# Hymba decoder layer: the first down-projection weights prepared inside the last FFN reading, the residual moved to the last block of pairs

## The chip, the cores and the metric

One core of a Trainium2 chip runs the whole layer. The metric is device time in microseconds (us), the median of some runs. TensorE (PE) multiplies, with its own weight loads (PEld) beside it; VectorE (DVE) and ScalarE (ACT) work on tiles; GpSimd (POOL) and SyncE (SP) here mainly issue DMA transfers, each from a queue in order.

## The reference, cut to what matters

1024 prompt tokens, 32 sample tokens and 16 meta tokens go through one layer: a mixer (short convolution and retention), then a SwiGLU FFN of width 2816, then a norm. The change lies in the FFN's down projection:

```python
x = x + jnp.concatenate([conv_out, ret_out], axis=-1) @ w_out
xn = _rmsnorm(x, norm2_g)
x = x + (jax.nn.silu(xn @ w_gate) * (xn @ w_up)) @ w_down      # w_down: 2816 x 1024
...
y_prompt = _rmsnorm(xp, final_norm_g)[:, N_META:]
```

`x` on the right of the second sum is called the residual here.

## The kernel before, in words

Everything is fp32, with features on the partitions and tokens along the free axis. The 1056 tokens that go through the FFN are two sets `s` (544 and 512), each of two groups `g`; group 0 of both sets together is 528 columns, and so is group 1. A matmul operand is split in two: a rounded high half (`whi`, `hh`, made by ACT as a copy to fp32r) and the rest (`wlo`, `hl`, made by DVE as a subtraction). A product then takes three matmuls per 128x128 weight tile: high by high, high by low, low by high. `split_u` splits weights into four rotating `whi` and four `wlo` buffers, so a split waits for the product four before it.

`strassen` multiplies a 2 x 2 block matrix of weights (a11, a12; a21, a22) by a 2 x 2 block matrix of activations with seven products instead of eight. Its weight sums are s3 = a11 + a21, s1 = a21 + a22, s2 = s1 + a11, s4 = s2 + a12 (the signs lie in the activations). The products are called y1 (a11 with b11), z1 (s3 with t3), y2 (s2 with t2), w1 (a12 with b21), y3 (s1 with t1), z2 (a22 with t4), y4 (s4 with b22). Three PSUM tiles y, z and u collect them: y2, y3 and y4 add into y, z2 into z. After each product the callback `on(step, ps)` reads the sum so far, so y2 can't start before the reading of y1 is done, y3 not before that of y2, y4 not before that of y3, z2 not before that of z1. In a matmul's name the PSUM tile is `by`, `bz`, `bw` in the FFN and `dy`, `dz`, `dw` in the down projection; `hb` and `ht` are the activations b11, b21, b22 and t1 to t4.

The FFN is read in 22 readings f, one for each 128 of its features: gate and up are the two rows, the token groups the two columns, and a product is 24 matmuls. Its `on` puts the parts together in `gt` and `up`; after the seven products ACT does Silu of `gt` and DVE multiplies by `up`. Results of readings 0 to 17 are combined in pairs and written to `hd` in DRAM, those of 18 to 21 (`spill_plain`) to `hp`; these writes are issued by POOL while the next reading runs, those of reading 21 after it.

The down projection takes the 18 paired tiles in four blocks of 2, 2, 2 and 3 pairs of them (`DBLOCKS`, `bi` 0 to 3). In a block, four calls of `strassen` follow each other, for output tiles m, m + 1 with m = 0, 2, 4, 6; a "pair" in this document is one such call. A product is 12 matmuls in blocks 0 to 2 and 18 in block 3. `x1[m][g]` are the 16 output tiles of 128 x 528 in SBUF. Before the change they hold the residual first: four are pulled when reading 21 begins, twelve during block 0, and all seven steps of each pair are DVE additions or subtractions into them:

```python
x = x1[m + i][g]
V.tensor_tensor(x, x, ps, ALU.subtract if i else ALU.add)
advance(ahead, step_n)
```

Activations are pulled from `hd` by SP (`pull_block`), one block ahead, a few with each step (`advance`); block 0's are pulled during reading 21, four with each of its steps. They lie in 62 `u` tiles of the pool `rows`, of which the FFN's own activations hold 56 until the product of reading 21 that reads them last is done. Weights come through `load_w` into five `wraw` buffers, on the same SP queue. After block 3 the four plain tiles are added in eight steps a group (`pd`), and the final norm follows.

The order on each engine is set by a scheduler that goes by the order of the code and by when it reckons buffers free; each queue then runs in that order, and an instruction that waits holds all behind it on its engine.

Of the kernel before, what the change touches and what calls it, by code (L numbers as in the profile page):

```python
# [10 lines left out]
F32 = mybir.dt.float32  # L11
F32R = mybir.dt.float32r
# [4 lines left out]
P = 128  # L17
# [101 lines left out]
def _body(nc, tc, t, offs, ncols):  # L119
# [3 lines left out]
    with contextlib.ExitStack() as ctx:  # L123
# [663 lines left out]

        def strassen(pool, a11, a21, a22, a12, n, kt, rhs, name, on):

            def total(nm, a, b):  # L790
                x = pool.tile([P, 512], F32, tag="ws", name=nm, bufs=4 if n > 384 else 2)
                V.tensor_tensor(x[:, :n], a[:, :n], b[:, :n], ALU.add)
                return x

            y, z, u = bank(name + "y"), bank(name + "z"), bank(name + "w")

            def product(ps, w, key, first):
                hi, lo = split_u(w, n)
                for s in range(SETS):
# [6 lines left out]

            product(y, a11, "b11", True)
            on("y1", cols(y))
            s3 = total("s3", a11, a21)
            product(z, s3, "t3", True)  # L810
            on("z1", cols(z))
            s1 = total("s1", a21, a22)
            s2 = total("s2", s1, a11)
            product(y, s2, "t2", False)
            on("y2", cols(y))
# [6 lines left out]
            on("z2", cols(z))  # L822
            product(y, s4, "b22", False)
            on("y4", cols(y))
# [11 lines left out]
        def spill(p, b11, b12, b21, b22):  # L836
# [22 lines left out]
            yield  # L859

        def spill_plain(i, b0, b1):
            for g, b in enumerate((b0, b1)):
                to_hd(hp[i, g], b[:, :HT], "h")
                yield
# [34 lines left out]
        def advance(gen, n):  # L899
            for _ in range(n):  # L900
                next(gen, None)

        pending = iter(())
        ahead = iter(())
# [3 lines left out]
        for f in range(NFF):  # L908
# [7 lines left out]
            if f == NFF - 1:  # L916
                for i in range(2):
                    for g in range(2):
                        x1[i][g] = pull(x1d[i, g], "x1", F32)[:, :HT]
                ahead = pull_block(0)  # L920

            def on(step, ps):
                if step == "y1":
                    S.activation(gt[0][:, :HT], ps, AF.Copy)
# [6 lines left out]
                elif step == "y3":  # L931
                    V.tensor_tensor(up[1][:, :HT], ps, up[1][:, :HT], ALU.add)
                elif step == "z2":
                    V.tensor_tensor(up[0][:, :HT], ps, up[0][:, :HT], ALU.add)
                else:
                    V.tensor_tensor(gt[1][:, :HT], ps, rstd2[1], ALU.mult)
                if f == 0 and step in ("y2", "w1"):
# [29 lines left out]
        for bi, (p0, p1) in enumerate(DBLOCKS):  # L967
# [13 lines left out]
            for m in range(0, KT, 2):  # L981
                w = nk * P
                at = 2 * p0 * P
                a11, a21 = (load_w(t["w_down"][m + i][:, at:at + w], w) for i in range(2))
                a22, a12 = (load_w(t["w_down"][m + i][:, at + w:at + 2 * w], w) for i in (1, 0))
                if bi == 0 and m > 0:
                    for i in range(2):
                        for g in range(2):
                            x1[m + i][g] = fin.tile([P, HT], F32, name=f"x1_{m + i}_{g}")
                            D.dma_start(x1[m + i][g], x1d[m + i, g])  # L990

                def on(step, ps):
                    i, g = {"y1": (0, 0), "z1": (1, 1), "y2": (1, 0), "w1": (0, 0), "y3": (1, 1), "z2": (1, 0),
                            "y4": (0, 1)}[step]
                    x = x1[m + i][g]
                    V.tensor_tensor(x, x, ps, ALU.subtract if i else ALU.add)  # L996
                    advance(ahead, step_n)

                strassen(fin, a11, a21, a22, a12, w, nk, dn_rhs, "d", on)

# [115 lines left out]
```

## Time and profile before

| | us |
|---|---|
| median of 3 runs | 1208.18 (1207.39 to 1209.49) |
| the profiled execution's own time | 1211.24 |
| its span, first to last instruction | 1209.5 |
| reading 21 of the FFN ends, block 0 begins | 951.8 |
| the third pair of block 0 begins | 982.3 |
| block 3's second pair begins | 1099.9 |
| last product of block 3 ends | 1145.9 |

Times within the span are us from its start. In rows of the profile, `out<-in` are the tiles by the program's names, `x12` is a count, and square brackets hold the idle time before the instruction on its engine and what ended it. A row `DMA wraw<-w_down` in the chain is a time in which the chain waited for that transfer.

### The profile page before, as it was taken

The numbers are of one execution on the slowest core, as the hardware profiler recorded it, in microseconds if no ns is written. First come the engines' busy times: TensorE is split into PE (matmuls) and PEld (weight loads), VectorE is DVE, ScalarE is ACT, GpSimd is POOL, SyncE is SP. The second block draws the span as 40 slices with busy tenths as digits, with TensorE's granted clock in tenths as the row PEclk, the third lists the DMA queues.
The fourth block names the chain that finished last, engine by engine and source line by source line (L and its number), as shares of the span: only waits on it lengthen the run. The fifth ranks groups of instructions, "written<-read, shape, count | busy, mean of one in ns | idle before, by whom it ended". The sixth has DMA issues, their size and how long they took to land.

```text
span 1209.5 us, 22838 instructions
## 1 busy us (share of the span) xinstructions
PE 1191.2 (98%) x8921; PEld 1138.3 (94%) x8921; DVE 843.8 (70%) x1591; ACT 487.7 (40%) x932; POOL 121.9 (10%) x251
## 2 busy tenths in 40 slices
PE   9999999999999999999999999999999899999997
PEld 8998988999989998899999999999999899999996
DVE  5455467676654577877887878787776588887656
ACT  7356531121233466545443444444444222222363
POOL 0100112000000012102211221122021000000000
PEclk9999999999999999999999999999999999999999
DMA  6221211100111355425434542454254998965213
GB/s 242 74 96 35 79 37 62 36 27 27 40 46 44 99 181 186 155 72 187 152 109 141 183 156 94 156 178 158 82 189 136 377 341 281 307 219 183 77 38 107
DMA packets 82059, 162.91 MB, mean 135 GB/s; under 512 B 10702, under 2 KB 23776, under 8 KB 81952
## 3 DMA queue, kind: packets, MB, share of 16 engines
q1 hardware_dynamic: 67424, 114.55, 29.1%
q0 software_dynamic: 14384, 46.88, 10.7%
q8 instruction: 70, 1.15, 0.4%
q14 instruction: 37, 0.30, 0.1%
q10 hardware_dynamic: 144, 0.02, 0.0%
HBM read 113.15 MB, written 48.26 MB: 133 GB/s over the span
## 4 chain that ended last, share of the span: by engine, by line
PE 96%; DMA 2%; ACT 1%; DVE 1%; issue 0%; SPq 0%; DVEq 0%; ACTq 0%
PE by L804 21%; PE bz L804 11%; PE dy L804 8%; PE po L186 8%; PE bw L804 5%; PE pk L186 4%; PE dz L804 4%; PE ph L186 4%; PE pc L186 4%; PE pd L1037 4%; PE pg L186 4%; PE pb L186 4%; PE pq L186 4%; PE pv L186 4%; PE dw L804 2%; PE po L604 1%
## 5 line engine op out<-in xcount | busy, mean ns | idle before, releaser
L158 ACT ACTIVATE whi<-wraw 128x512 fp32r<-128x512 f32 (+2 forms) x198 | 115.7, 584 | 283.2 <-issue 60.0
L160 DVE TENSOR_TENSOR wlo<-wraw,whi 128x512 fp32r<-128x512 f32 (+2 forms) x198 | 124.3, 628 | 48.1 <-ACT whi L158 47.9
L158 ACT ACTIVATE whi<-s 128x512 fp32r<-128x512 f32 (+2 forms) x152 | 83.5, 551 | 159.5 <-PE by L804 46.1
L804 PE MATMUL by<-t,whi 128*128 128x256 f32 (+1 forms) x704 | 130.3, 284 | 0.0
L804 PE MATMUL bz<-t,whi 128*128 128x256 f32 (+1 forms) x704 | 130.1, 284 | 0.0
L804 PE MATMUL by<-b,whi 128*128 128x256 f32 (+1 forms) x704 | 129.2, 283 | 0.0
L160 DVE TENSOR_TENSOR wlo<-s,whi 128x512 fp32r<-128x512 f32 (+2 forms) x152 | 89.3, 588 | 35.5 <-ACT whi L158 34.5
L804 PEld LDWEIGHTS by<-b,whi 128*128 128x128 f32 x704 | 109.1, 188 | 0.1
L804 PEld LDWEIGHTS bz<-t,whi 128*128 128x128 f32 x704 | 109.1, 188 | 0.0
L804 PEld LDWEIGHTS by<-t,whi 128*128 128x128 f32 x704 | 108.8, 188 | 0.1
L804 PE MATMUL bz<-t,wlo 128*128 128x256 f32 (+1 forms) x352 | 100.0, 284 | 0.0
L804 PE MATMUL by<-b,wlo 128*128 128x256 f32 (+1 forms) x352 | 100.0, 284 | 0.0
L804 PE MATMUL by<-t,wlo 128*128 128x256 f32 (+1 forms) x352 | 99.7, 283 | 0.0
L804 PEld LDWEIGHTS bz<-t,wlo 128*128 128x128 f32 x352 | 66.4, 189 | 0.0
L804 PEld LDWEIGHTS by<-b,wlo 128*128 128x128 f32 x352 | 66.3, 188 | 0.0
L804 PEld LDWEIGHTS by<-t,wlo 128*128 128x128 f32 x352 | 66.1, 188 | 0.0
L804 PE MATMUL bw<-b,whi 128*128 128x272 f32 (+1 forms) x352 | 65.4, 285 | 0.0
L996 DVE TENSOR_TENSOR x<-x,dy 128x528 f32<-128x528 f32 x64 | 45.0, 703 | 27.1 <-PE dy L804 26.2
L830 POOL DMA_DIRECT2D hd<-hh x63 | 33.9, 540 | 268.6 <-ACT hh L828 263.2
L804 PE MATMUL dz<-ht,whi 128*128 128x256 f32 (+1 forms) x288 | 54.3, 285 | 3.6 <-ACT whi L158 3.6
L804 PE MATMUL dy<-hb,whi 128*128 128x256 f32 (+1 forms) x288 | 54.7, 289 | 2.7 <-ACT whi L158 2.7
L804 PE MATMUL dy<-ht,whi 128*128 128x256 f32 (+1 forms) x288 | 54.9, 288 | 0.0
(305 smaller groups left out, 3100.4 us busy)
## 6 DMA issues: line engine op xcount, KB each, us to landing
ht<-hd SPq DMA_DIRECT2D x72, 264.0 KB, 5.1
hd<-hh POOLq DMA_DIRECT2D x63, 264.0 KB, 3.8
hd<-hl POOLq DMA_DIRECT2D x63, 264.0 KB, 3.9
hb<-hd SPq DMA_DIRECT2D x54, 264.0 KB, 5.2
wraw<-w_in SPq DMA_DIRECT2D x54, 256.0 KB, 2.6
wraw<-w_gate SPq DMA_DIRECT2D x44, 256.0 KB, 2.6
wraw<-w_up SPq DMA_DIRECT2D x44, 256.0 KB, 2.9
wraw<-w_out SPq DMA_DIRECT2D x32, 256.0 KB, 2.7
```

Source lines behind the costliest of these rows:

```text
L158: S.activation(hi[:, :n], raw[:, :n], AF.Copy)
L160: V.tensor_tensor(lo[:, :n], raw[:, :n], hi.bitcast(F32)[:, :n], ALU.subtract)
L186: T.matmul(ps[:, g, :n], wt[:, sl], xk[part][:, g * n:(g + 1) * n], start=(first and i == 0), stop=(last and i == 2))
L604: T.matmul(po[:, h, :], pms[hh][:, j, :], vt[c][:, b, h * HD:(h + 1) * HD], start=False, stop=(hh == 1))
L804: T.matmul(out, wt[:, sl], rhs(s, k, key, part), start=(first and k == 0 and i == 0), stop=(k == kt - 1 and i == 2), skip_group_check=not ...
L830: G.dma_start(dst[0], hi.bitcast(F32)[:, :HT])
L996: V.tensor_tensor(x, x, ps, ALU.subtract if i else ALU.add)
L1037: T.matmul(ps[:, 0, :n], wt[:, sl], hs[k][g][part][:, SO[s]:SO[s] + n], start=(k == 0 and i == 0), stop=(k == NPL - 1 and i == 2))
```

## The change

Three things are done. First, when reading 21 has read z1 and y2, SP loads a11, a21, a22 and a12 of the first two pairs of block 0 into eight `u` tiles (`dw`); and at a new step "ready" of reading 21, between its z2 and y4, `prepare` makes the first pair's sums s3, s1, s2 and the splits of a11, s3 and s2. `tc.issue_after` then puts the eviction of reading 21's y4 behind the last of these splits on DVE, and the first pair's evictions behind them on DVE and ACT. Second, `x1` no longer begins as the residual: in block 0 the steps y1, z1, y2 and y4, which are the first to reach their tile, are ACT copies (with scale -1 for odd i), and the residual is loaded in block 3 (`res`, four rotating buffers that belong to the output staging tag `yt`) and added by DVE behind the same four steps of each pair. Third, the four `hp` stores of reading 21 are issued by SP after the first pair's code, and no longer by POOL.

```diff
+        def prepare(a11, a21, a22, n):
+            w1 = split_u(a11, n)
+            s3 = wsum(rows, "s3", a11, a21, n)
+            w2 = split_u(s3, n)
+            s1 = wsum(rows, "s1", a21, a22, n)
+            s2 = wsum(rows, "s2", s1, a11, n)
+            hi, lo = (wts.tile([P, 512], F32R, tag=tag, name=tag) for tag in ("whi", "wlo"))
+            act = S.activation(hi[:, :n], s2[:, :n], AF.Copy)
+            last = V.tensor_tensor(lo[:, :n], s2[:, :n], hi.bitcast(F32)[:, :n], ALU.subtract)
+            return last, act, w1, w2, (hi, lo), s1, s2
...
             for g, b in enumerate((b0, b1)):
-                to_hd(hp[i, g], b[:, :HT], "h")
+                if i < NPL - 1:
+                    to_hd(hp[i, g], b[:, :HT], "h")
+                else:
+                    waiting.extend(zip((hp[i, g, 0], hp[i, g, 1]), split_x(b[:, :HT], HT, "h")))
...
             if f == NFF - 1:
-                for i in range(2):
-                    for g in range(2):
-                        x1[i][g] = pull(x1d[i, g], "x1", F32)[:, :HT]
                 ahead = pull_block(0)
...
+                if step == "ready":
+                    if f == NFF - 1:
+                        down_ready.extend(prepare(*down_w[0][:3], 2 * P))
+                    return
...
-                    V.tensor_tensor(gt[1][:, :HT], ps, rstd2[1], ALU.mult)
+                    with tc.issue_after(down_ready[0].ins) if down_ready else contextlib.nullcontext():
+                        V.tensor_tensor(gt[1][:, :HT], ps, rstd2[1], ALU.mult)
+                if f == NFF - 1 and step in ("z1", "y2"):
+                    m = 0 if step == "z1" else 2
+                    n = 2 * P
+                    for i, a in ((0, 0), (1, 0), (1, 1), (0, 1)):
+                        x = ut("dw")
+                        D.dma_start(x[:, :n], t["w_down"][m + i][:, a * n:(a + 1) * n])
+                        down_w[m].append(x)
...
+                res = [[None] * 2 for _ in range(2)]
+                if bi == len(DBLOCKS) - 1:
+                    for i in range(2):
+                        for g in range(2):
+                            res[i][g] = fin.tile([P, SG], F32, tag="yt", name="res", bufs=4)[:, :HT]
+                            D.dma_start(res[i][g], x1d[m + i, g])
...
-                    V.tensor_tensor(x, x, ps, ALU.subtract if i else ALU.add)
+                    first = step in ("y1", "z1", "y2", "y4")
+                    with contextlib.ExitStack() as order:
+                        if bi == 0 and m == 0:
+                            order.enter_context(tc.issue_after(down_ready[0].ins))
+                            order.enter_context(tc.issue_after(down_ready[1].ins))
+                        if bi == 0 and first:
+                            S.activation(x, ps, AF.Copy, scale=-1.0 if i else 1.0)
+                        else:
+                            V.tensor_tensor(x, x, ps, ALU.subtract if i else ALU.add)
+                    if first and res[i][g] is not None:
+                        V.tensor_tensor(x, x, res[i][g], ALU.add)
                     advance(ahead, step_n)
...
+                strassen(fin, a11, a21, a22, a12, w, nk, dn_rhs, "d", on,
+                         down_ready[2:] if bi == 0 and m == 0 else None)
+                while waiting:
+                    dst, x = waiting.pop(0)
+                    D.dma_start(dst, x.bitcast(F32)[:, :HT])
```

The scheduler's order on DVE, from the last work on group 0 of reading 21 on, before. The fourth row reads y1 of the first pair:

```order
L949 SCALAR_TENSOR_TENSOR up_10551<-up_10551,gt_10549 128x528
L936 TENSOR_TENSOR gt_10550<-by_10561,rstd2_3951 128x528
L949 SCALAR_TENSOR_TENSOR up_10552<-up_10552,gt_10550 128x528
L996 TENSOR_TENSOR x1_10553<-x1_10553,dy_10874 128x528
L829 TENSOR_TENSOR hl_10851<-up_10551,hh_10850 128x528
L829 TENSOR_TENSOR hl_10857<-up_10552,hh_10856 128x528
L792 TENSOR_TENSOR s3_10896<-wraw_10866,wraw_10868 128x256
L792 TENSOR_TENSOR s1_10917<-wraw_10868,wraw_10870 128x256
L160 TENSOR_TENSOR wlo_10900<-s3_10896,whi_10898 128x256
L792 TENSOR_TENSOR s2_10919<-s1_10917,wraw_10866 128x256
L160 TENSOR_TENSOR wlo_10923<-s2_10919,whi_10921 128x256
```

And after:

```order
L986 SCALAR_TENSOR_TENSOR up_10551<-up_10551,gt_10549 128x528
L793 TENSOR_TENSOR s3_10822<-dw_10630,dw_10632 128x256
L793 TENSOR_TENSOR s1_10828<-dw_10632,dw_10634 128x256
L793 TENSOR_TENSOR s2_10830<-s1_10828,dw_10630 128x256
L160 TENSOR_TENSOR wlo_10826<-s3_10822,whi_10824 128x256
L805 TENSOR_TENSOR wlo_10833<-s2_10830,whi_10832 128x256
L966 TENSOR_TENSOR gt_10550<-by_10553,rstd2_3951 128x528
L160 TENSOR_TENSOR wlo_10942<-dw_10636,whi_10940 128x256
L160 TENSOR_TENSOR wlo_10961<-s1_10828,whi_10959 128x256
L986 SCALAR_TENSOR_TENSOR up_10552<-up_10552,gt_10550 128x528
L160 TENSOR_TENSOR wlo_10982<-dw_10634,whi_10980 128x256
L171 TENSOR_TENSOR hl_10877<-up_10551,hh_10876 128x528
```

The sums s3, s1, s2 and two splits moved ahead of `gt<-by`, the eviction of reading 21's y4; the reading of the first pair's y1 left this engine.

ACT, from the split of a11 on, before:

```order
L158 ACTIVATE whi_10877<-wraw_10866 128x256
L947 ACTIVATE gt_10549<-gt_10549 128x528
L947 ACTIVATE gt_10550<-gt_10550 128x528
L828 ACTIVATE hh_10850<-up_10551 128x528
L828 ACTIVATE hh_10856<-up_10552 128x528
L158 ACTIVATE whi_10898<-s3_10896 128x256
L158 ACTIVATE whi_10921<-s2_10919 128x256
```

And after, down to the reading of y2's sum:

```order
L984 ACTIVATE gt_10550<-gt_10550 128x528
L158 ACTIVATE whi_10980<-dw_10634 128x256
L170 ACTIVATE hh_10876<-up_10551 128x528
L170 ACTIVATE hh_10880<-up_10552 128x528
L1050 ACTIVATE x1_10888<-dy_10892 128x528
L1050 ACTIVATE x1_10891<-dz_10893 128x528
L158 ACTIVATE whi_10999<-s4_10978 128x256
L158 ACTIVATE whi_11029<-dw_10685 128x256
L1050 ACTIVATE x1_10890<-dy_10892 128x528
```

The splits of s3, s2, a12 and s1 now stand ahead of the Silu of group 1 (`gt_10550`), and the new copies of y1 and z1 (`x1<-dy`, `x1<-dz`) behind both `hh`. On PE the first pair's products now come as y1, z1, w1, y2, eight matmuls of z2, y3, the other four, four of the next pair's y1, y4; before, they came as y1, z1, y2, w1, y3, z2, y4.

SP in block 3, from the weights of its second pair on, before:

```order
L153 DMA wraw<-w_down 128x384 x4
L873 DMA hp<-hp 128x528 x7
L153 DMA wraw<-w_down 128x384 x3
L873 DMA hp<-hp 128x528 x2
L153 DMA wraw<-w_down 128x384 x5
```

And after:

```order
L153 DMA wraw<-w_down 128x384 x4
L1036 DMA res<-x1d 128x528 x3
L900 DMA hp<-hp 128x528 x7
L1036 DMA res<-x1d 128x528
L153 DMA wraw<-w_down 128x384 x4
```

The fourth residual load of a pair, which waits for a buffer until the pair before is done, now stands ahead of the weights of the pair that follows.

More of the change, by code (lines that the diff above doesn't have):

```diff
@@ L805, in product @@
                                      stop=(k == kt - 1 and i == 2), skip_group_check=not first)
-            product(y, a11, "b11", True)
+            product(y, ready[0] if ready else a11, "b11", True)
             on("y1", cols(y))
-            s3 = total("s3", a11, a21)
-            product(z, s3, "t3", True)
+            product(z, ready[1] if ready else total("s3", a11, a21), "t3", True)
             on("z1", cols(z))
-            s1 = total("s1", a21, a22)
-            s2 = total("s2", s1, a11)
-            product(y, s2, "t2", False)
+            if ready:
+                w3, s1, s2 = ready[2:]
+            else:
+                s1 = total("s1", a21, a22)
+                w3 = s2 = total("s2", s1, a11)
+            product(y, w3, "t2", False)
             on("y2", cols(y))
@@ L822, in strassen @@
             on("z2", cols(z))
-            product(y, s4, "b22", False)
+            w7 = split_u(s4, n)
+            on("ready", None)
+            product(y, w7, "b22", False)
             on("y4", cols(y))
@@ L859, in spill @@
             yield
+        waiting = []
         def spill_plain(i, b0, b1):
             for g, b in enumerate((b0, b1)):
-                to_hd(hp[i, g], b[:, :HT], "h")
+                if i < NPL - 1:
+                    to_hd(hp[i, g], b[:, :HT], "h")
+                else:
+                    waiting.extend(zip((hp[i, g, 0], hp[i, g, 1]), split_x(b[:, :HT], HT, "h")))
                 yield
@@ L901, in advance @@
                 next(gen, None)
+        down_w, down_ready = {0: [], 2: []}, []
         pending = iter(())
@@ L983, in _body @@
                 at = 2 * p0 * P
-                a11, a21 = (load_w(t["w_down"][m + i][:, at:at + w], w) for i in range(2))
-                a22, a12 = (load_w(t["w_down"][m + i][:, at + w:at + 2 * w], w) for i in (1, 0))
-                if bi == 0 and m > 0:
+                if bi == 0 and m in down_w:
+                    a11, a21, a22, a12 = down_w[m]
+                else:
+                    a11, a21 = (load_w(t["w_down"][m + i][:, at:at + w], w) for i in range(2))
+                    a22, a12 = (load_w(t["w_down"][m + i][:, at + w:at + 2 * w], w) for i in (1, 0))
+                if bi == 0:
                     for i in range(2):
                         for g in range(2):
-                            x1[m + i][g] = fin.tile([P, HT], F32, name=f"x1_{m + i}_{g}")
-                            D.dma_start(x1[m + i][g], x1d[m + i, g])
+                            x1[m + i][g] = (ut("x1")[:, :HT] if m == 0 else
+                                            fin.tile([P, HT], F32, name=f"x1_{m + i}_{g}"))
+                res = [[None] * 2 for _ in range(2)]
[4 more added lines that the diff above has]
+                            D.dma_start(res[i][g], x1d[m + i, g])
                 def on(step, ps):
+                    if step == "ready":
+                        return
                     i, g = {"y1": (0, 0), "z1": (1, 1), "y2": (1, 0), "w1": (0, 0), "y3": (1, 1), "z2": (1, 0),
```

16 lines of the change are left out of this document (10 added, 6 removed).

## The prediction

> **What bounds the kernel now.** I read the page's busy shares and the shares of its chain first.
>
> ```profile
> PE 1191.2 (98%) x8921; PEld 1138.3 (94%) x8921; DVE 843.8 (70%) x1591; ACT 487.7 (40%) x932; POOL 121.9 (10%) x251
> PE 96%; DMA 2%; ACT 1%; DVE 1%; issue 0%; SPq 0%; DVEq 0%; ACTq 0%
> ```
>
> PE is the bound, and only what is not a PE piece in the chain can be won by moving other work. Next, who keeps PE waiting (us in total, times, longest), and the chain in order of time (start, us, what) around the only long interruption:
>
> ```profile
> PE dz L804 <- ACT whi L158: 3.6, 1, 3.6
> PE dy L804 <- ACT whi L158: 2.7, 1, 2.7
> PE pk L186 <- ACT xnh L173: 1.7, 1, 1.7
> ```
>
> ```profile
> 937.38 2.92 PE by L804 x24
> ...
> 948.69 5.57 DMA ht<-hd
> ...
> 954.32 5.56 DMA wraw<-w_down
> ...
> 960.51 6.92 DMA wraw<-w_down
> ...
> 967.45 0.43 DVE s L792
> ...
> 980.84 2.90 PE dy L804 x24
> 991.02 2.90 PE dy L804 x24
> 1001.19 2.91 PE dy L804 x24
> ```
>
> The two large waits both lie in the first pair of the down projection: product z1 waits for the split of s3, whose weights w_down came late behind the queue of transfers, and y4 waits for s4, whose a12 came later still. The last three rows are each the y4 of one pair and the y1 of the next: an undisturbed pair takes 1001.19 - 991.02 = 10.17 us, 1.453 per product. The idle time is not all of the price; chosen stretches say what follows it (us from and to, length, busy us of PE, PEld, DVE, ACT and POOL, then the granted clock, where 1.00 is full, DMA share and GB/s):
>
> ```profile
> 7.00:10.00 3.00, 1.78 (x9) 1.62 (x10) 1.16 (x2) 1.92 (x4) 0.00 (x0) 0.92 1.03 374
> 10.00:13.00 3.00, 3.00 (x12) 2.72 (x11) 2.12 (x5) 3.00 (x6) 0.00 (x0) 0.51 1.02 383
> 958.40:961.70 3.30, 3.30 (x17) 3.30 (x16) 2.47 (x6) 1.02 (x3) 0.00 (x0) 0.50 0.99 361
> 969.00:972.00 3.00, 2.96 (x13) 2.99 (x14) 1.69 (x4) 0.53 (x2) 0.00 (x0) 0.50 1.05 380
> ```
>
> After each of the waits (3.6, 2.7, and 1.7 at the kernel's start) PE runs about 3.3 us at half clock, so 1.65 us more is lost.
>
> **What there is to win.** The first down matmul, and the rows that give my prices:
>
> ```profile
> 951.79 0.42 PE L804 MATMUL dy<-hb,whi 128*128 128x272 f32 x2
> ```
>
> ```profile
> 950.64 0.71 DVE L949 SCALAR_TENSOR_TENSOR up<-up,gt 128x528 f32<-128x528 f32 x1
> 951.99 0.71 DVE L936 TENSOR_TENSOR gt<-by,rstd 128x528 f32<-128x528 f32 x1 [0.64 <-PE by L804]
> 956.00 0.76 DVE L792 TENSOR_TENSOR s<-wraw 128x256 f32<-128x256 f32 x2
> 956.99 0.43 DVE L160 TENSOR_TENSOR wlo<-s,whi 128x256 fp32r<-128x256 f32 x1 [0.23 <-ACT whi L158]
> 957.45 0.42 DVE L792 TENSOR_TENSOR s<-s,wraw 128x256 f32<-128x256 f32 x1
> 940.81 0.59 ACT L928 ACTIVATE up<-by 128x528 f32<-128x528 f32 x1
> 952.73 0.64 ACT L947 ACTIVATE gt<-gt 128x528 f32<-128x528 f32 x1 [7.13 <-DVE gt L936]
> 954.15 0.64 ACT L828 ACTIVATE hh<-up 128x528 fp32r<-128x528 f32 x1 [0.24 <-DVE up L949]
> 956.54 0.42 ACT L158 ACTIVATE whi<-s 128x256 fp32r<-128x256 f32 x1 [1.75 <-DVE s L792]
> ```
>
> From 951.79, thirteen products of 1.453 would put y4 of the second pair at 970.68. It starts at 980.84: 10.2 us are lost here, 6.3 of them idle and the rest half clock. That is the most that the change can bring.
>
> **The change, part by part.**
>
> *Down weights loaded in the last FFN reading, sums and splits ahead of it (gain 10.2).* Eight loads of 128 KB go out after z1 and y2 of f = 21, into u tiles. In time: the first four wait only for the u tiles that y1 of f = 21 reads (seven products of 2.92 end at 951.79, so y1 ends near 934.3), and are needed at 943 (a11) and 951 (the others). The sums and splits of s3, s1, s2 now stand on DVE behind the last scalar_tensor_tensor of group 0 (row 950.64, ends 951.35), so they are not really ahead, but early enough: s3 to 951.7, s1 to 952.0, s2 (needs s1) to 952.5, at 0.42 each with the overlap of the pair at 956.00; ACT's half of s3 to 952.2, DVE's half to 952.8, both before z1 would start (951.79 + 1.45 = 953.24). So z1 no longer waits. a12 is in SBUF by then, so y4 doesn't wait for a load either.
>
> *The eviction of the last y4 is held behind down_ready (a wait added, cost 0.8).* It runs when the low half of s2 is done: ACT's half of s2 ends 953.0, DVE's 953.45, so gt<-by goes 953.4 to 954.1 instead of 951.99 to 952.70. Behind it in order: Silu to 954.75 (0.64), the scalar_tensor_tensor to 955.5, ACT's hh of group 1 to 956.2, and only then the new ACT copy of y1, 0.59, to 956.7. PE now runs the products y1, z1, w1 (951.79 to 956.15) and then y2, which adds into the bank that this copy reads: it waits 956.7 - 956.15 = 0.55. The copy of y2's sum stands behind the splits of s4 and of the next a11 on ACT; y2 ends 958.15, the copy 959.35, while PE fills the time with eight of z2's twelve matmuls (0.97, to 959.1): 0.25 more. Sum 0.8. The wait can't be below nothing; its upper bound is the 2.7 of the row above.
>
> *First block copied by ACT instead of added by DVE (0).* 16 evictions of 0.59 go to ACT and 16 of about 0.7 leave DVE; neither bounds this stretch once the weights are there. In the second quiet pair, ACT has room (row 982.30 below: 5.38 of 20.4).
>
> *x1 leaves block 0's queue (0, perhaps a gain).* Twelve loads of 264 KB go from the busiest DMA stretch. PE had no wait for them there, so I book nothing.
>
> *hp stores of the last reading, POOL to SP (0).* Four issues; the first waits on SP for hh of group 0 (about 955.7), and behind it stand the loads for block 1. The rows on the queue:
>
> ```profile
> 951.49 2.71 SPq L873 DMA_DIRECT2D hb<-hd  x4
> 955.00 2.44 SPq L873 DMA_DIRECT2D hb<-hd  x4
> 978.44 3.42 SPq L873 DMA_DIRECT2D ht<-hd  x5
> ht<-hd SPq DMA_DIRECT2D x32, 264.0 KB, 5.6
> x<-x1d SPq DMA_DIRECT2D x12, 264.0 KB, 4.2
> ```
>
> One pull goes out per 0.69 us and lands after 5.6. Ahead of the fourth pair's a21 stand 4 stores and 21 pulls: 25 x 0.69 = 17.2, so it is issued at 973 and lands near 979. In the new schedule the third pair begins at 951.79 + 14 x 1.453 + 0.8 = 972.9; DVE reaches the sum that needs a21 at about 978.0, and a DVE held by it hurts PE only when the third pair's y3 eviction comes later than y4's start, 972.9 + 6 x 1.453 = 981.6. Cost 0 with some 2 us to spare. If a pull costs as much as 0.85 (24 loads of 264 KB and 7 small ones went out between 955.00 and 978.44 before), it lands at 982.6, and up to 2 us are lost: the bound. The eight new loads also stand ahead of block 0's own pulls. b22's last one went out at 954.2 (951.49 + 2.71) and landed near 959.8; eight half loads of 0.35 would make it 962.6, and y4 of the first pair wants it at 951.79 + 6 x 1.453 + 0.8 = 961.3. So 0 to 1.3; I take 0, because these pulls now get u tiles of an earlier product (b21's) and needn't be issued so late.
>
> *Residual in the last block (0).* Sixteen loads of 264 KB and sixteen DVE adds of at most 0.71 on two SBUF operands. Rows of the second half of block 0 and of the second pair of the last block, then DVE in that pair:
>
> ```profile
> 982.30:1002.70 20.40, 20.40 (x170) 20.40 (x170) 16.86 (x36) 5.38 (x14) 0.00 (x0) 1.00 0.99 335
> 1099.00:1114.50 15.50, 15.50 (x130) 15.50 (x129) 10.35 (x18) 3.68 (x7) 0.00 (x0) 1.00 0.31 101
> ```
>
> ```profile
> 1099.91 0.70 DVE L996 TENSOR_TENSOR x<-x,dy 128x528 f32<-128x528 f32 x1 [1.01 <-PE dy L804]
> 1100.53 0.55 DVE L160 TENSOR_TENSOR wlo<-wraw,whi 128x384 fp32r<-128x384 f32 x1
> 1102.10 0.70 DVE L996 TENSOR_TENSOR x<-x,dy 128x528 f32<-128x528 f32 x1 [1.02 <-PE dy L804]
> 1104.38 0.70 DVE L996 TENSOR_TENSOR x<-x,dz 128x528 f32<-128x528 f32 x1
> 1106.48 0.71 DVE L996 TENSOR_TENSOR x<-x,dy 128x528 f32<-128x528 f32 x1 [0.94 <-PE dy L804]
> ```
>
> Four more adds make DVE 10.35 + 4 x 0.71 = 13.2 of 15.5: below PE. Products take 2.19 here and DVE idles about 1 us ahead of most evictions, which is where an add fits. The loads have four buffers: the one for (1, 1) of a pair waits for the add of (0, 1) of the pair before, at 1099.91 + 0.7 + 0.55 + 0.7 = about 1101.8, lands 4.2 later at 1106.0, and DVE asks for it at 1105.5 (z1's eviction and one split). DVE then loses 0.5; PE would wait only if y2's eviction (1106.5) came after 1108.0, when y3 needs the bank. So nothing, with 1.5 us to spare.
>
> **Sum.** 10.2 - 0.8 = 9.4 us. The profiled execution took 1211.24 (span 1209.5), 3.1 above the median of 1208.18; I expect its like at 1201.8, span 1200.1, and the median at 1208.18 - 9.4 = 1198.8.
>
> **Rivals.**
>
> *Half clock after the short waits.* The stretch 7 to 10 us was idle for 1.2 of 3.0 and the next one ran at 0.51. The new waits are 0.55 and 0.25 within 3 us, about a quarter. Against it: less idle than any case seen here. For it: the threshold isn't shown. Once costs 1.65, twice 3.3: 1200.5 to 1202.1. The Trainium skill, TensorE: Matmul & The Clock Gate, Part 1, has the clock halved only after an idle window of about 3.4 us, by which 0.8 us costs nothing more; the waits of 2.7 and 1.7 above, shorter than that, were followed by 0.50 and 0.51, so the trace does not bear it out. The same page, in "A second HAM failure mode", tells of short idles between groups of matmuls that set the clock swinging, which would speak for this rival.
>
> *The fourth pair's weights, or the tiles for b22, come late.* DMA is the reserve that was used up: its share is 0.99 to 1.05 in the rows above. Up to 2 us as worked out for the weights, 1.3 for b22: 1200.8, with both 1202.1. Against it: 3.2 MB of x1 are gone from this stretch.
>
> *Slower: residual loads stall the last block.* The load of (1, 1) goes out when the pair before is done, with the next pair's w_down behind it on SP. Up to 4.2 + 2.0 = 6.2 us of landing time cost PE nothing (the 0.5 and 1.5 above); each us beyond is paid in three pairs. To eat up 9.4 it needs 6.2 + 3.1 = 9.3 us, and to end 0.2% above before (2.4 more) 10.1: 1210.6. The slowest kind of load above takes 5.6, and DMA is at 0.31 in this stage, so it is unlikely.
>
> *It doesn't do what it says.* If z1 still waits, because the weights' u tiles are freed later than I read, the transition stays as it is: 1208. Against it: they wait for y1 and z1 of f = 21 and for two stores of f = 20.
>
> **Chances.** 0.2% is 2.4 us, near the spread of the three runs (1207.39 to 1209.49), and what this can tell from no change. As worked out 0.58; half clock 0.18; late transfers 0.15; no effect 0.05; slower 0.04. The first three all end faster by over 0.2%: 0.91, same 0.05, slower 0.04. The range goes from all 10.2 won with 0.8 of spread (1197.2) to a half-clock or late-transfer case with a little of the other (1203.0).
>
> **What would show it.** Right: no PE wait above 1 us between 951 and 985; y4 of the second pair (the chain's pair of 24) near 971.5; y2 of the first pair waiting about half a us for an ACT copy; granted clock 1.00 throughout; the chain without a w_down piece; the last block's pairs still 15.3 us each (2.19 a product). Wrong: stretches at 0.5 after 956; a PE wait on ACT whi near 981; DVE waiting for res by more than 2 us and PE for DVE in the last block.

## The result, and the profile after

The changed kernel takes 1200.83 us (median; 1199.88 to 1201.97) against 1208.00 before (1207.39 to 1209.49): ratio 0.9939, 95% interval 0.9925 to 0.9953, so 7.2 us less. Forecast: 1198.8, 9.4 less, range 1197.2 to 1203.0. The profiled execution took 1199.88, span 1198.0.

Busy shares and chain shares after:

```profile
PE 1185.9 (99%) x8921; PEld 1133.0 (95%) x8921; DVE 844.1 (70%) x1591; ACT 496.0 (41%) x948; POOL 119.7 (10%) x247
PE 95%; DMA 2%; DVE 1%; ACT 1%; issue 0%; SPq 0%; DVEq 0%; ACTq 0%
```

What PE waits for (us in total, times, longest; three waits that are as before are left out, 1.1 at the kernel's start, 1.6 and 0.3 behind block 3); the waits of 3.6 and 2.7 are gone, and three of about half a us are new, the rows with `dy`:

```profile
PE dy L822 <- ACT whi L158: 0.6, 1, 0.6
PE pk L186 <- ACT xnh L173: 0.6, 1, 0.6
PE dy L822 <- ACT x L1050: 0.5, 1, 0.5
PE dy L822 <- DVE x L1052: 0.4, 1, 0.4
```

The two profiled spans differ by 11.5, more than the medians, because of the kernel's start, which the change doesn't touch. The clock column (third from the end) of the same two us, first before, then after:

```profile
9.00:11.00 2.00, 2.00 (x9) 1.69 (x9) 1.40 (x3) 2.00 (x5) 0.00 (x0) 0.63 0.98 393
```

```profile
9.00:11.00 2.00, 2.00 (x14) 1.76 (x13) 1.70 (x4) 2.00 (x5) 0.00 (x0) 1.00 1.01 397
```

In the execution before, the start's wait of 1.7 was followed by half clock; after, the same wait was 0.6 and the clock stayed full. Over all kernels of this study the first down matmul begins between 947.28 and 951.79, in no order that follows the edits. So the comparison below goes by an inner stretch, called **the measure**: from the first down matmul to the first matmul of the plain tiles (`pd`). It comes from the one profiled execution of each kernel, and how much it varies between executions of one kernel was not recorded. PE's rows, first before (its first down matmul, 951.79, stands in the prediction; the first row here is y4 of the second pair), then after:

```profile
980.68 0.29 PE L804 MATMUL dy<-hb,whi 128*128 128x272 f32 x1
...
1145.69 0.29 PE L1037 MATMUL pd<-hp,wdh 128*128 128x272 f32 x1
```

```profile
947.28 0.28 PE L822 MATMUL dy<-hb,whi 128*128 128x272 f32 x1
...
967.38 0.29 PE L822 MATMUL dy<-hb,whi 128*128 128x272 f32 x1
...
1133.83 0.29 PE L1099 MATMUL pd<-hp,wdh 128*128 128x272 f32 x1
```

Measure before 193.90, after 186.55: 7.35 won, as in the medians. Up to y4 of the second pair it was 28.89 before and is 20.10 after: 8.79 won there. So 1.44 is given back later. The chain after shows where: transfers stand in it between 958 and 976, and the step from the second pair's y4 (967.38) to the third's (978.14), 10.17 undisturbed, is 10.76.

```profile
958.15 5.68 DMA hp<-hl
963.89 6.73 DMA hb<-hd
970.69 4.98 DMA wraw<-w_down
978.14 3.20 PE dy L822 x24
```

### The profile page after: what moved, and what is told of

It is laid out like the page before. It is cut to its first block, busy times and chain, and to the rows that moved or that the text cites. A ratio compares the mean times of both kernels' runs of the same rounds, so it can differ in the third digit from the quotient of the medians.

```text
span 1198.0 us, 22826 instructions
## 1 busy us (share of the span) xinstructions
PE 1185.9 (99%) x8921; PEld 1133.0 (95%) x8921; DVE 844.1 (70%) x1591; ACT 496.0 (41%) x948; POOL 119.7 (10%) x247
## 4 chain that ended last, share of the span: by engine, by line
PE 95%; DMA 2%; DVE 1%; ACT 1%; issue 0%; SPq 0%; DVEq 0%; ACTq 0%
PE by L822 21%; PE bz L822 11%; PE dy L822 8%; PE po L186 8%; PE bw L822 5%; PE ph L186 4%; PE pc L186 4%; PE pd L1099 4%; PE pk L186 4%; PE pg L186 4%; PE pb L186 4%; PE pq L186 4%; PE dz L822 4%; PE pv L186 4%; PE dw L822 2%; PE po L604 1%
## 5 line engine op out<-in xcount | busy, mean ns | idle before, releaser
L158 ACT ACTIVATE whi<-wraw 128x512 fp32r<-128x512 f32 (+2 forms) x192 | 113.2, 590 | 279.3 <-issue 54.8
L822 PEld LDWEIGHTS bw<-b,whi 128*128 128x128 f32 x352 | 54.4, 188 | 0.0
```

The source lines that it names most:

```text
L158: S.activation(hi[:, :n], raw[:, :n], AF.Copy)
L822: T.matmul(out, wt[:, sl], rhs(s, k, key, part), start=(first and k == 0 and i == 0), stop=(k == kt - 1 and i == 2), skip_group_check=not ...
```

## How the two large waits of before are to be read

The prediction read both waits of the first pair as waits for that pair's weights. The trace of before says otherwise, and the experiments follow from that. First DVE and PE at the wait of 2.72 (the bracket names ACT's `whi`), then two splits of ACT, the last one for the first pair before the wait and the only one within it:

```profile
967.45 0.87 DVE L792 TENSOR_TENSOR s<-wraw 128x256 f32<-128x256 f32 x2 [2.97 <-DMA wraw<-w_down]
968.24 0.70 DVE L996 TENSOR_TENSOR x<-x,dy 128x528 f32<-128x528 f32 x1
```

```profile
969.04 0.56 PE L804 MATMUL dy<-hb,whi 128*128 128x272 f32 x1 [2.72 <-ACT whi L158]
```

```profile
962.09 0.42 ACT L158 ACTIVATE whi<-s 128x256 fp32r<-128x256 f32 x1 [2.51 <-PE dy L804]
...
967.99 0.42 ACT L158 ACTIVATE whi<-s 128x256 fp32r<-128x256 f32 x1 [4.20 <-DVE s L792]
```

s4's high half was ready at 962.5 and its low half, made by DVE, at 963.0, long before. What ends 0.1 ahead of PE's start is DVE's eviction of y3 (968.24 + 0.70 = 968.94), and that stood behind a sum that waited 2.97 for weights: those of the **second** pair. The `whi` that the bracket names can only be the split at 967.99, which is of the second pair's s3 and which y4 doesn't use; so the bracket is not to be trusted here. The wait of 3.6 for z1 has no late weights either: DVE reached s3 at 956.00 with no wait for a transfer, right behind the last multiplication of reading 21, the eviction of y1 and both `hl` of reading 21, which end at 955.97:

```profile
954.65 1.32 DVE L829 TENSOR_TENSOR hl<-up,hh 128x528 fp32r<-128x528 f32 x2
```

So the **order theory**: z1 waited for the queue order on DVE and ACT, y4 for an eviction behind another pair's late sum. The rival is the prediction's **load theory**: both waited for the first pair's own weights.

## The experiments

All measures in one table; ratios are against the kernel before, run beside it (its median was 1207.48 to 1207.73 beside kernels 1 to 12).

| kernel | median | ratio (95% interval) | first down matmul | first pd matmul | measure |
|---|---|---|---|---|---|
| before | 1208.00 | 1 | 951.79 | 1145.69 | 193.90 |
| after | 1200.83 | 0.9939 (0.9925 to 0.9953) | 947.28 | 1133.83 | 186.55 |
| 1 loads, no prepare | 1203.97 | 0.9971 (0.9962 to 0.9980) | 948.03 | 1137.30 | 189.27 |
| 2 second pair's loads only | 1209.37 | 1.0015 (1.0005 to 1.0025) | 947.82 | 1140.80 | 192.98 |
| 3 prepare, residual in block 0 | 1209.16 | 1.0016 (1.0006 to 1.0025) | 949.36 | 1143.07 | 193.71 |
| 4 residual moved only | 1205.41 | 0.9983 (0.9971 to 0.9995) | 949.95 | 1139.41 | 189.46 |
| 5 w_down on POOL | 1199.56 | 0.9929 (0.9915 to 0.9943) | 949.21 | 1134.13 | 184.92 |
| 6 w_down in two transfers | 1200.51 | 0.9937 (0.9925 to 0.9950) | 948.85 | 1133.76 | 184.91 |
| 7 no hold | 1201.43 | 0.9951 (0.9939 to 0.9964) | 947.82 | 1135.87 | 188.05 |
| 8 hp stores on POOL | 1201.12 | 0.9948 (0.9935 to 0.9960) | 950.24 | 1136.76 | 186.52 |
| 9 first pair ahead of hh | 1201.30 | 0.9944 (0.9932 to 0.9957) | 947.91 | 1135.26 | 187.35 |
| 10 twelve unread loads | 1203.36 | 0.9962 (0.9949 to 0.9974) | 948.83 | 1137.44 | 188.61 |
| 11 before, w_down on POOL | 1205.43 | 0.9982 (0.9973 to 0.9992) | 948.55 | 1139.78 | 191.23 |
| 12 as 9, hh in a gap | 1198.18 | 0.9922 (0.9908 to 0.9936) | 951.05 | 1135.08 | 184.03 |

**1. Loads without prepare.**

```diff
                 if step == "ready":
-                    if f == NFF - 1:
-                        down_ready.extend(prepare(*down_w[0][:3], 2 * P))
                     return
```

> The changed kernel without prepare and without issue_after: the eight dw loads, the ACT copies in block 0 and the residual in block 3 stay; the first pair's sums and splits are made in the usual order. Measure: from the first down matmul to the first pd matmul, 193.90 us before and 186.55 after. Order theory (z1's wait of 3.6 in the kernel before was the queue of DVE and ACT, where the last Silu, both hh and both hl stand ahead of s3; its weights had landed long before): z1 still waits about 3.1 (3.6 less 0.6, since the copy of y1 left DVE) and half clock follows, 1.65, against 1.2 lost there after the change; y4 of the first pair no longer waits. The measure is then about 190 and the time about 1204. Load theory (the prediction's words: both waits are for the first pair's weights): z1 doesn't wait either, the time is that of the changed kernel, 1200 to 1201.

PE's only wait in blocks 0 to 3, and the stretch behind it:

```profile
PE dz L822 <- ACT whi L158: 3.2, 1, 3.2
```

```profile
952.80:956.10 3.30, 3.24 (x18) 3.08 (x19) 2.67 (x7) 1.95 (x6) 0.00 (x0) 0.73 1.05 399
```

z1 waits 3.2 with its weights in SBUF: the order theory holds, at the size it gave (measure 189.27, 190 expected). y4 no longer waits.

**2. The second pair's loads alone, in the kernel before.**

```diff
+                if f == NFF - 1 and step == "y2":
+                    for i, a in ((0, 0), (1, 0), (1, 1), (0, 1)):
+                        x = ut("dw")
+                        D.dma_start(x[:, :n], t["w_down"][2 + i][:, a * n:(a + 1) * n])
+                        down_w.append(x)
...
+                if bi == 0 and m == 2:
+                    a11, a21, a22, a12 = down_w
```

> The kernel before with one thing added: the second pair's four weights are loaded in reading 21 into u tiles. First pair, residual and evictions as before. Order theory (y4 of the first pair waited for the eviction of y3, which stood on DVE behind the second pair's s3, which waited 2.97 for the second pair's a21): y4's wait of 2.7 and the half clock behind it go, 4.4 in all; z1 still waits 3.6. Time about 1203.6. Load theory (y4 waits for the first pair's own s4 and a12): y4 waits as before, and the four loads ahead of the pulls can only make it later: 1208 or more.

```profile
PE dy L804 <- DVE x L1006: 2.8, 1, 2.8
```

```profile
973.04 0.87 DVE L792 TENSOR_TENSOR s<-wraw 128x256 f32<-128x256 f32 x2 [3.16 <-DMA wraw<-w_down]
```

z1 waits 3.6 as before. The first pair's y4 runs without a wait, so its wait was indeed for the second pair's a21. But a wait of 2.8, now labelled with DVE's eviction, appears one pair later (at 975.62), behind the third pair's sum, the DVE row above. Both theories missed the time: mine expected 4.4 less. The profiled execution was the fastest of this kernel and its measure is 0.9 below before; the median is 1.9 above, and what the other executions lost, one trace doesn't show.

**3 and 4. The change's two halves alone.** Kernel 3 is the changed kernel with the residual loaded and added in block 0 again, and hp stores on POOL; kernel 4 is the kernel before with only the residual moved and block 0's first evictions as ACT copies. Against the changed kernel, 3 and then 4:

```diff
+                            D.dma_start(x1[m + i][g], x1d[m + i, g])
...
-                if bi == len(DBLOCKS) - 1:
+                if False:
...
-                        if bi == 0 and first:
+                        if False:
```

```diff
-                        down_ready.extend(prepare(*down_w[0][:3], 2 * P))
...
-                if f == NFF - 1 and step in ("z1", "y2"):
+                if False and step in ("z1", "y2"):
```

> The changed kernel with the residual as before (x1 loaded in reading 21 and block 0, every step a DVE add there, nothing added in block 3) and hp stores on POOL. If the transfers bound this stretch (DMA share 0.97 from 948 to 990 after the change): twelve loads of 264 KB more in block 0, some 0.69 us each; eight of them stand ahead of the fourth pair's weights, so these come about 5 later, DVE is held by the fourth pair's s3, and PE loses 4 to 6: measure about 191 to 192, time 1205 to 1207. If those loads were hidden anyway: as the changed kernel, 1200 to 1201, or a little less since y1's copy no longer stands on ACT behind hh.

> The kernel before with the residual moved to block 3 and ACT copies in block 0, without dw loads, prepare or issue_after; hp stores on POOL. Order theory: z1 waits about 3.1 and half clock follows (2.0 to 2.2 less than nothing is won: 0.6 gained at most); the second pair's a21 stands some five transfers earlier on SP, about 3.4, since the four x1 pulls are gone and seven pulls come later, so DVE is not held and y4's 4.4 is won: time about 1203. If moving the residual were worth nothing by itself: 1208. A cost in block 3 would show as pairs over 15.33 there.

Kernel 3, PE's two longest waits, then DVE at the largest and the stretch behind it:

```profile
PE dy L822 <- DVE x L1052: 2.3, 1, 2.3
PE dz L822 <- DMA ht<-hd: 1.6, 2, 1.4
```

```profile
968.50 0.70 DVE L1052 TENSOR_TENSOR x<-x,dy 128x528 f32<-128x528 f32 x1 [2.29 <-DMA x<-x1d]
```

```profile
969.20:972.50 3.30, 3.25 (x19) 3.25 (x20) 2.84 (x6) 0.42 (x1) 0.00 (x0) 0.69 1.06 375
```

In blocks 0 to 3 of kernel 4 PE has one wait, z1's, with the same row as in kernel 1 (3.2).

Prepare and early loads alone win 0.2 of the measure and lose 1.7 in the time: z1 starts at once, but the pulls for t4 come 1.4 late and DVE stands 2.29 at a residual tile that hasn't landed. The residual alone wins 4.4 (y4's wait, and 0.4 of z1's), though its median falls by only 2.1. SP's order tells how: the second pair's a21 goes out 4.6 behind the first down matmul instead of 8.7, since one pull and one residual load stand between it and the a11 ahead of it, where there were seven pulls. First before, where a21 is the first of three loads, then kernel 4:

```profile
960.51 3.19 SPq L153 DMA_DIRECT2D wraw<-w_down  x3
```

```profile
954.51 0.33 SPq L153 DMA_DIRECT2D wraw<-w_down  x1
```

The twelve x1 loads of block 0 stood behind that a21 before (the first at 964.20), so they can't have delayed it. Together the two halves win 7.35, more than the sum of both. I had expected kernel 3 to lose 4 to 6 of the gain; it lost all of it, 7.2.

**10. The loads themselves.** Is that the transfers, or the evictions that read them?

```diff
+                if bi == 0 and m > 0:
+                    for i in range(2):
+                        for g in range(2):
+                            D.dma_start(fin.tile([P, SG], F32, tag="yt", name="idle", bufs=4)[:, :HT], x1d[m + i, g])
```

> The changed kernel with twelve loads of 264 KB more in block 0, of the residual into four rotating tiles that nobody reads, at about the place where the x1 loads stood. Evictions, sums and their order on DVE and ACT stay. It asks whether the kernel with prepare but the residual in block 0 lost its gain to those loads alone (measure 193.7 there, 186.55 after the change). Transfer theory: 191 to 194, with DVE waiting for w_down and PE for DVE or for ht. Eviction theory (it was DVE's additions and their order): 186.5 to 188.

```profile
PE dz L822 <- ACT whi L158: 1.0, 1, 1.0
PE dy L822 <- ACT whi L158: 1.0, 1, 1.0
```

```profile
979.98 0.77 DVE L793 TENSOR_TENSOR s<-wraw 128x256 f32<-128x256 f32 x2
...
982.80 0.41 ACT L158 ACTIVATE whi<-s 128x256 fp32r<-128x256 f32 x1
```

188.61: 2.1 of the 7.2 are paid with unread loads alone, above the eviction theory's range and below the transfer theory's. But the order on DVE and ACT did not stay as it was, which the expectation had taken for granted. The rows above show the first of the two waits. The fourth pair's first sum, which after the change stands ahead of the third pair's w1 eviction (DVE at 975.76, below), here stands behind that of z2; it is made at 979.98 with no wait, its a21 having gone out 26.1 behind the first down matmul instead of 23.4. ACT's split of it comes only at 982.80, behind the new copy of y1, and z1 waits 1.0 for it, at 983.26. So the 2.1 are the later weights together with the order that the scheduler then chose, and this run doesn't separate them. The other 5.1 appear only where a residual tile is read in block 0 (with four more loads in reading 21, and another order on DVE); these parts weren't separated either.

**5, 6, 8 and 11. The late weights: place in the queue or full DMA engines?** After the change, PE waits 0.36 at 978.14 and 0.63 at 1037.29. PE, and DVE ahead of it:

```profile
978.14 0.39 PE L822 MATMUL dy<-hb,whi 128*128 128x272 f32 x1 [0.36 <-DVE x L1052]
...
1037.29 0.36 PE L822 MATMUL dy<-ht,whi 128*128 128x272 f32 x1 [0.63 <-ACT whi L158]
```

```profile
975.76 0.42 DVE L793 TENSOR_TENSOR s<-wraw 128x256 f32<-128x256 f32 x1 [1.52 <-DMA wraw<-w_down]
...
977.39 0.70 DVE L1052 TENSOR_TENSOR x<-x,dy 128x528 f32<-128x528 f32 x1
...
1036.09 0.43 DVE L793 TENSOR_TENSOR s<-wraw 128x256 f32<-128x256 f32 x1 [1.28 <-DMA wraw<-w_down]
1036.48 0.70 DVE L1052 TENSOR_TENSOR x<-x,dy 128x528 f32<-128x528 f32 x1
```

Both are the mechanism of y4 once more: a sum waits for a21, the eviction behind it ends at most 0.1 ahead of PE's start (977.39 + 0.70, 1036.48 + 0.70; the label `whi` is again not the one).

Kernel 5 (and 11, the same edit in the kernel before), where `q` is POOL for w_down:

```diff
-            D.dma_start(raw[:, :n], ap)
+            (q or D).dma_start(raw[:, :n], ap)
```

Kernel 6, in blocks 0 to 2:

```diff
+                    r0, r1 = (load_w(t["w_down"][m + i][:, at:at + 2 * w], 2 * w) for i in range(2))
+                    a11, a12, a21, a22 = r0[:, :w], r0[:, w:], r1[:, :w], r1[:, w:]
```

> The changed kernel, with the four w_down loads of every later pair issued by POOL, whose queue is idle here, instead of SP behind the pulls. After the change two waits of PE are left in blocks 0 to 2, 0.36 at 978.1 and 0.63 at 1037.3; at both DVE had stood 1.52 and 1.28 at a sum whose a21 landed late. Queue theory (the loads are late because of their place in SP's queue): both waits go, the measure from the first down matmul to the first pd matmul falls from 186.55 to about 185.0, the time by 1.5 against the changed kernel. Bandwidth theory (the DMA engines are full, share 0.97, so some transfer is late whatever the order): a wait for a pull or for weights stays or takes their place; 186 to 188.

> The changed kernel, with a pair's w_down in two transfers of 128 x 512 instead of four of 128 x 256 in blocks 0 to 2, each in one wraw tile: half the transfers of that kind, and five tiles hold two and a half pairs, so the loads go out about a pair earlier. Both theories of the late weights: the sums of the fourth pair and of block 1 find their weights, both waits go, measure about 185.0, time 1.5 below the changed kernel. If bandwidth alone counts (the bytes are the same): as the changed kernel, 186 to 187.

Both waits go in both kernels, and both land on 184.9: the late weights cost 1.6 of the measure. The medians fall by 1.3 and 0.3, less than the 1.5 expected, and their intervals overlap with that of the changed kernel, so the times alone wouldn't show it. DMA's share from 949 to 990 is 1.03 in kernel 5 and 0.97 after the change, so the engines are no less full; the order in the queue decided. In kernel 5 POOL issued the fourth pair's second load (a21) 17.5 behind the first down matmul, as soon as a DVE sum of the third pair had freed a buffer for it. After the change the same sum ended 17.2 behind, but SP got to that load only at 970.69, 23.4 behind. First kernel 5, then after the change:

```profile
966.71 0.54 POOL L153 DMA_DIRECT2D wraw<-w_down  x1 [29.19 <-DVE s L793]
```

```profile
970.69 1.67 SPq L153 DMA_DIRECT2D wraw<-w_down  x3
```

The Trainium skill, DMA: Bandwidth & Descriptors, section "Issuing engines are not separate DMA queues", says that issuing from several engines only saves the issuing time, usually small beside the transfer. Here it saved 1.6, because SP's queue holds a load back until the pulls ahead of it are out, and these wait for earlier pulls to land (SP's waits, 940 to 1045 us, after):

```profile
SPq L900 <- DMA ht<-hd: 10.7, 24, 2.0
```

Kernel 8 undoes the third part of the change:

```diff
-                if i < NPL - 1:
-                    to_hd(hp[i, g], b[:, :HT], "h")
-                else:
-                    waiting.extend(zip((hp[i, g, 0], hp[i, g, 1]), split_x(b[:, :HT], HT, "h")))
+                to_hd(hp[i, g], b[:, :HT], "h")
```

> The changed kernel with the four hp stores of reading 21 on POOL again. The scheduler then puts three of block 3's residual loads on SP in their place, about where the stores stood. Queue theory of the fourth pair's weights: one transfer less ahead of them, 0.7 earlier, so the wait of 0.36 at 978 halves; measure 186.2 to 186.5. Bandwidth theory: three loads of 264 KB more in the full stretch, the weights come up to 2 later, DVE and PE lose as much; measure 187.5 to 188.5. In the last block no change either way.

186.52, as after the change: three residual loads took the place of the stores and the weights went out as late as before. So the third part of the change, as the scheduler orders the queue around it, costs nothing and wins nothing; what the stores alone cost on SP isn't shown.

> The kernel before with all w_down loads of blocks 0 to 3 issued by POOL. Queue theory: the second pair's a21 lands before DVE asks for it, y4's wait of 2.7 and the half clock behind it go, z1's wait of 3.6 stays (DVE's order); measure 189 to 190, time about 4 below before. Transfer theory (with the x1 loads in block 0 the engines are full, so something else is late in their place): a wait for ht, hb or w_down of 1 to 4 within the first three pairs, measure 191 to 194, time within 2 of before.

```profile
PE dz L804 <- ACT whi L158: 3.6, 1, 3.6
PE dy L804 <- issue: 1.7, 1, 1.7
```

2.7 won, and neither theory is whole. y4's wait is gone, as the queue theory has it, but the measure lies at the low end of the transfer theory's range (191 to 194), and something else was late in its place: the second pair's a21 now stood on POOL behind four hp stores that waited for hl and went out at 953.99; DVE then stood 2.79 at a sum, until 960.64, with y2's eviction behind it, and y3 waited 1.65 for that bank. (The row's "issue" names no releaser; the place on DVE is what speaks for the weights.) Its z1 still waits 3.6.

**7. The hold.** `issue_after` taken off, in both places:

```diff
-                    with tc.issue_after(down_ready[0].ins) if down_ready else contextlib.nullcontext():
+                    with contextlib.nullcontext():
```

> The changed kernel without issue_after (both uses), so DVE does the eviction of reading 21's y4 and the multiplication of group 1 first and the sums s3, s1, s2 behind them; loads, prepare and residual as after the change. If the hold is what lets z1 start at once: s3 about 1.5 later, z1 waits some 1.7 and half clock may follow (1.65 more), while y2's wait of 0.55 for the ACT copy shrinks; measure 188 to 189.5, time 1 to 3 above the changed kernel. If the hold only costs (the 0.8 that the prediction booked): measure 185.5 to 186, time about 0.8 below.

```profile
PE dz L822 <- ACT whi L158: 1.6, 1, 1.6
```

```profile
951.00:954.30 3.30, 3.16 (x23) 2.94 (x24) 2.39 (x7) 2.29 (x7) 0.00 (x0) 1.00 0.80 305
```

The hold is worth 1.5: z1 waits 1.6 without it (1.7 expected), without half clock behind it. Up to y4 of the second pair the loss is 2.2; 0.7 of it come back later, most of it because the wait at the third pair's y4 is gone.

**9 and 12. What is left in the first pair.** From the first down matmul to its y4 the first pair takes 9.74 after the change instead of 6 x 1.453 = 8.72. Kernel 9 is kernel 5 with the first pair's code ahead of reading 21's hh and hl; kernel 12 also asks for them at z1 (the last two lines), and sums s4 early:

```diff
+        ahead, step_n = start(0)
+        down_pair(0, DBLOCKS[0][0], DBLOCKS[0][1] - DBLOCKS[0][0], 0, parts[0], rows)
         for _ in pending:
             pass
         late_ctx.close()
...
+                if bi == 0 and m == 0 and step == "z1":
+                    advance(pending, 2)
```

> The changed kernel with w_down loads on POOL and the first pair's code written ahead of the last drain of pending, so that ACT copies y1, z1 and y2 before it makes hh of reading 21, and DVE makes hl behind the evictions. If the rest of the loss in the first pair (9.74 from the first down matmul to the first y4, against 6 x 1.453 = 8.72, so 1.0) is the copy of y1 standing behind both hh on ACT: y2's wait of 0.54 and what follows it go, measure 184.0 to 184.2, time about 0.8 below the kernel with only the POOL loads. If it is the wait for DVE's held sums or the copy itself: 184.9 as there. Against both: the plain stores and the output tiles of the second pair wait longer for hh and hl; a wait there would bring back up to 1.

```profile
960.22 1.33 DVE L171 TENSOR_TENSOR hl<-up,hh 128x528 fp32r<-128x528 f32 x2 [1.80 <-ACT hh L170]
961.59 0.76 DVE L793 TENSOR_TENSOR s<-dw 128x256 f32<-128x256 f32 x2
```

A miss in the time, and it tells the most: the first pair fell to 8.98, so the copy of y1 behind both hh was its loss; but hl then stood ahead of the second pair's s3, whose z1 waited 2.4.

> The kernel in which the first pair's code stands ahead of the last drain of pending, with two more moves: hh of reading 21 is asked for right after the copy of z1 (ACT is free there for 1.5) and s4 of the first pair is summed ahead of y2, so that hl goes on DVE behind w1's eviction, where it was idle for 2.9, and no longer ahead of the second pair's sums. If the wait of 2.41 in that kernel was only hh and hl standing in front of the second pair's s3: it goes, the first pair stays at 8.98, measure 184.0 to 184.2, time about 0.8 below the kernel with only the POOL loads. If these four instructions can't be hidden anywhere in the first two pairs: a wait of 0.5 or more for ACT or DVE remains, measure 184.9 or more.

```profile
1135.08 0.29 PE L1109 MATMUL pd<-hp,wdh 128*128 128x272 f32 x1
```

The first pair takes 8.74, no PE wait is left in blocks 0 to 3, and the measure is 184.03 (184.0 to 184.2 expected). The median of kernel 12, 1198.18, is the lowest of the study, 2.7 below the changed one (2.1 by the ratios); the intervals of the two overlap, as do those of kernels 12 and 5, so it is the measure that ranks them.

## Why the prediction was right, point by point

*The gain of the transition, 10.2 less 0.8.* 28.89 - 13 x 1.453 = 10.0 were there to win, 8.79 were won. The size was right, the reason was not: "z1 waits for the split of s3, whose weights w_down came late" and "y4 waits for s4, whose a12 came later still" are both refuted (kernels 1 and 2). That the number held is luck as far as the reason goes: the change happens to remove the true causes too. Prepare and the hold put s3 ahead of reading 21's last work, and y4's cause is removed twice: the second pair's weights are among the eight early loads (kernel 2 shows what that does), and moving the residual alone brings them in time as well (kernel 4).

*The held eviction, 0.8.* The wait for the copy of y1 is 0.55, exactly as worked out from the queue:

```profile
952.36 0.40 PE L822 MATMUL dy<-ht,whi 128*128 128x272 f32 x1 [0.55 <-ACT x L1050]
```

```profile
952.30:955.60 3.30, 3.24 (x25) 3.14 (x26) 2.73 (x7) 1.73 (x5) 0.00 (x0) 1.00 1.02 351
```

The 0.25 that was booked for the copy of y2's sum doesn't appear as a wait of PE. The whole came to 1.0 in the first pair and 1.2 by the second's y4; the products around a wait run 0.1 to 0.2 longer (y2 1.58, y3 1.56). Half clock did not follow in this execution, nor in any other profiled one behind a wait of 0.3 to 1.0 in these blocks, so that rival did not come true.

*x1 leaves block 0 (0, perhaps a gain).* The worst-sized term. Alone it wins 4.4, and without it the rest wins nothing. I took "PE had no wait for them" as a price of zero, but moving the residual also takes four pulls out of reading 21 and gives SP another order, and that is what brought the second pair's a21 out 4.2 earlier. Twelve such loads in block 0 cost 2.1 in kernel 10, together with the order that came with them.

*The fourth pair's weights (0, bound 2).* This rival came true in part. The load went out 23.4 behind the first down matmul, where 973 - 951.79 = 21.2 was worked out, and landed 28.4 behind, where harm was to begin at 29.8. The limit was wrong: DVE, 1.52 late, had four instructions, the sum first, in front of y3's eviction. From one y4 to the next PE took 10.76 there and 10.34 in the pair behind it instead of 10.17, and, in a place I hadn't looked at, the first pair of block 2, 11.09.

*Stores on SP (0), residual in the last block (0).* Right: kernel 8 is equal, and the chain's y3 pieces of block 3 after the change are 15.34 apart (15.33 before), and DVE has no wait for a residual tile there.

```profile
1081.40 2.20 PE dy L822 x18
...
1096.74 2.20 PE dy L822 x18
```

*The sum.* 9.4 forecast, 7.35 measured: 8.79 won by y4 of the second pair, where 10.0 - 0.8 = 9.2 were forecast by the same count, less 1.44 given back later, of which late weights are the cause that the runs show (kernels 5 and 6). Of the signs that were to show it, "no w_down piece in the chain" failed, and it pointed at the term that was off.

## What to carry to other kernels

Before a wait is put down to a transfer, look at what ended just ahead of the waiting instruction's start, and at what stands in front of that on its engine: here one queue that runs in order, DVE's, turned the late weights of one pair into waits of the pair ahead of it, once before the change, twice after it, and again in kernel 2. A load that nobody waits for isn't free: it can stand in a queue ahead of loads that somebody will need, and the order of other engines can change around it (kernel 10). And two edits that each remove one of several causes must be timed together: one half won 4.4 of the measure, the other 0.2, both 7.35. Work that is pushed back (hh and hl here) has to be followed to the gap where it fits, or the wait only moves to the next pair.

## What the runs showed of the hardware that I had not expected

Half clock after a wait is no function of the wait's length alone. After the five waits of 3.15 to 3.6 in the down projection the next 3.3 us had a mean clock of 0.58 to 0.76; of the shorter ones, 2.72 (before, first pair) and 2.32 and 1.39 (kernel 3) were followed by 0.53, 0.69 and 0.70, but 2.79 (kernel 2), 2.41 (kernel 9), 1.65 (kernel 11) and 1.63 (kernel 7) by 1.00, and so were all of 0.3 to 1.0 in blocks 0 to 3. Kernel 2's stretch behind its 2.79:

```profile
975.60:979.00 3.40, 3.38 (x28) 3.40 (x29) 2.86 (x7) 1.09 (x3) 0.00 (x0) 1.00 1.05 376
```

At the kernel's start two waits of the same place and nearly the same length differ as well: 1.24 in kernel 4 was followed by half clock, 1.23 in kernel 11 was not (the same two us, first kernel 4, then kernel 11):

```profile
9.00:11.00 2.00, 2.00 (x8) 1.72 (x8) 1.69 (x3) 2.00 (x5) 0.00 (x0) 0.51 1.02 418
```

```profile
9.00:11.00 2.00, 2.00 (x10) 1.29 (x10) 1.68 (x3) 2.00 (x5) 0.00 (x0) 1.00 1.00 406
```

The Trainium skill, TensorE: Matmul & The Clock Gate, Part 1, halves the clock after at least one idle window of about 3.4 us. That fits the waits of 3.6 and the shorter ones at full clock, and not those from 1.24 to 3.2 that were followed by half clock. What sets these apart from the others is open.

DMA engines at a share of 1.03 (kernel 5, 949 to 990) made PE wait for nothing but the copy of y1, while at 0.97 after the change PE waited for late weights: what decided was which transfer stood first.
